# Order of a two-layer decoder's fp32r kernel on one core: formed weight blocks kept behind the sums, strict product order in the last two blocks, last key copies first, third row block's output operands earlier

## The chip, the cores and the metric

One NeuronCore of a Trainium2 chip runs the whole program. The metric is the device time of one execution in microseconds (us); the kernel before took 2277.39 us (median of 3 runs, 2275.31 to 2277.57). Less is better. A measurement of this kernel can tell about 0.2% (4.6 us) from no change.

## What is computed

Two layers over 1024 tokens of width 1024 in fp32. Layer 0 mixes by latent attention (8 heads), layer 1 by differential attention (8 heads with two softmax maps each); after each stands a gated feed-forward of inner width 5632.

```python
for i in range(DEPTH):                      # 2
    mix = _mla_mixer(h, ...) if i % 2 == 0 else _diff_mixer(h, ...)
    h = _layernorm(ALPHA * h + mix, ln_mix_g[i], ln_mix_b[i])
    h = _layernorm(ALPHA * h + _swiglu(h, ffn_w_gu[i], ffn_w_down[i]), ln_ffn_g[i], ln_ffn_b[i])

def _swiglu(x, w_gu, w_down):
    gate, up = jnp.split(x @ w_gu, 2, axis=-1)
    return (jax.nn.silu(gate) * up) @ w_down

def _diff_mixer(x, ...):                    # cut
    a = p[:, 0] - lam * p[:, 1]             # p: two softmaxes over the same mask
    o = jnp.einsum('bhqk,bkhe->bqhe', a, v)
    o = _rmsnorm(o, g_sub) * (1.0 - lambda_init)
    return o.reshape(b, s, DIFF_HEADS * DIFF_V) @ w_o
```

## The kernel before

Every fp32 product is done as three fp32r matmuls: each operand is cut into a high part (a cast, on ACT) and a low part (operand less high part, on DVE or POOL), and high by high, high by low and low by high are summed in PSUM. An `op_` tile holds both parts of one weight piece. A product of four 128-row steps is 12 matmuls of 512 columns; the text calls it a unit.

**Stages**, by time in the profile: attention of layer 0 to about 345 us; its output projection to 450; gate and up product of feed-forward 0 to 871; its down product to 1086; attention of layer 1 to 1550; the rest of its output projection to 1624; gate and up of feed-forward 1 to 2044; down to the end.

**Gate and up product** (`ffn`). The weight is cut into 22 blocks n of 4 pieces (a11, a12, a21, a22: one 1 MB load `gr`, issued on SP's queue by `load`, L563). Each block takes seven units, called 1 to 7 by the `pr` of `product`, in a scheme that trades one of eight products for sums of weight pieces and of inputs. `prepare(n, pr)` forms the weight sums in place on DVE (L585, L587, L589) and the tile `s3` (L593), then cuts the piece in two (`op_unit`, L514 and L515). `consume(n, pr)` runs the unit into a PSUM tile `ga`, `gb` or `gc` and adds the result into `tmp` or `pg` on DVE (L633 to L645). `gb` is one bank: unit 7 may not write it before DVE has added unit 6's result. The inputs of the units are `xs["t1"]`, `["t2"]`, `["t3"]`, `["t4"]`, `["b22"]` (in the trace `t3h_f` and so on). `stream` lists the units and `prepare` is called four units ahead of `consume`. The first six blocks' units 1 and 2 run early (`gates`, from loads `gp` by `load_pre`, tiles `gp`/`op_gp`/`pg`). `pending` is the transposition of the last row block of the output projection (`raw_x`, PE tiles `xTp_a`).

**The order** on each engine is set ahead of time by a scheduler that simulates the program with its own costs, priorities and tile slots; each engine then runs its list strictly in that order. SP's list is the DMA queue: a load that waits holds back those behind it. `behind(i, j)` pins instruction i after j. `big_tile` gives one of six 1 MB slots, shared by `gr`, `pg`, `hp`, `sh` and others.

**Down product.** `t2` subtracts two weight tiles in place (`tt`, DVE) and cuts the result; `from_h` cuts the activations (`op_h`).

**Attention of layer 1.** `proj_b` makes a head's queries and keys; keys are copied as high part on ACT (`bk`, L1350) and low part on DVE (L1351), in two column halves `hf` and two map halves `mp`. `score_b` (`s_b`) and the softmax (`l_b` exponentials, L227) follow; row blocks of the last head go in `LAST_ORDER` = 6, 7, 4, 5, 2, 3, 0, 1. `OutProj` begins the output projection under the last head: `of` loads six heads' outputs of a row block (`of_a`), and cuts them into `oh_a`, `ol_a` (ACT L405, DVE L406); `product` runs them against the weights `wo`, `who`, `wlo` into `zp_a`; `rest` finishes the row blocks, of the third and later ones also the cutting.

Of the kernel before, what the change touches and what calls it, by code (L numbers as in the profile page):

```python
# [12 lines left out]
ALU = mybir.AluOpType  # L13
# [3 lines left out]
P = 128  # L17
# [25 lines left out]
def trunk(  # L43
# [84 lines left out]
    def load_w(src, cols, name, hi=None, lo=None, eng=None, raw=None, ins=False):  # L128

        if raw is None:  # L130
            raw = wp.tile([P, 1024], F32, tag="wr", bufs=2, name=f"r_{name}")
        nc.sync.dma_start(raw[:, :cols], src)
        if hi is None:
            hi = wp.tile([P, 1024], F32R, tag="wh", name=f"h_{name}")
            lo = wp.tile([P, 1024], F32R, tag="wl", name=f"l_{name}")
        A.copy(hi[:, :cols], raw[:, :cols])
        j = (eng or G).tensor_tensor(lo[:, :cols], raw[:, :cols], f32(hi[:, :cols]), ALU.subtract)
        return (hi, j.ins) if ins else (hi, lo)

# [7 lines left out]
    def tr(ps_out, in_):  # L147
        T.transpose(ps_out, in_, ident)

# [135 lines left out]
    def out_proj(side, w_o, o_dram, x_src, x_dst, lng, lnb, xo):  # L285


        with tc.tile_pool(name="op0", bufs=2, side=side, reuse_waits="tile") as pool:
# [21 lines left out]
            for tb in LAST_ORDER:  # L310
# [34 lines left out]
                prev = (tb, y)  # L345
        return lambda: raw_x(prev[1], xo, prev[0], f"a0_{prev[0]}")

    class OutProj:
# [24 lines left out]

        def of(self, tb):

# [10 lines left out]
            else:  # L386
# [13 lines left out]
            self.sums[tb] = small(f"sum_{nm}", 2)  # L400
            self.split(tb, slice(0, n), of)

        def split(self, tb, hs, o):
            oh, ol = (t[:, hs] for t in self.oh[tb])
            A.activation(oh, o, AF.Copy, scale=self.scale)  # L405
            V.scalar_tensor_tensor(ol, o, self.scale, f32(oh), ALU.mult, ALU.subtract)  # L406
# [37 lines left out]
        def rest(self, lng, lnb, xo):  # L444
# [15 lines left out]
            self.st.close()  # L460
            return lambda: raw_x(self.z[prev], xo, prev, f"a1_{prev}")

    def raw_x(y, xo, tb, name):

# [4 lines left out]
        for kh in range(2):  # L469
            pt = ps_s(f"xTp_{name}_{kh}")  # L470
            for k in range(4):
                tr(pt[:, k * P:(k + 1) * P], y[:, (4 * kh + k) * P:(4 * kh + k + 1) * P])
            pv = pt.rearrange("p (k t) -> p k t", k=4)
# [6 lines left out]
        if tb < 4:  # L480
# [40 lines left out]
    def ffn(side, xo, xst, pending, layer, x_src, x_dst, lng, lnb, next_x, spare=()):  # L521
# [43 lines left out]
        def load_pre(n, eng):  # L565
# [7 lines left out]
        begun = set()  # L573

        def prepare(n, pr):


            if n not in begun:
                begun.add(n)
                load(n + 1)  # L580
                if n < npre - 1:
                    load(n + 2)
            a11, a12, a21, a22 = (r[n][:, i] for i in range(4))
            if pr == ("5" if n < 2 else "6"):
                V.tensor_tensor(a21, a21, a22, ALU.add)  # L585
            if pr == ("3" if n < 2 else "6"):
                V.tensor_tensor(a11, a21, a11, ALU.subtract)  # L587
            if pr == "3":
                V.tensor_tensor(a12, a12, a11, ALU.subtract)  # L589
# [8 lines left out]
            eng = V if n < 2 else eng  # L598
            ops[n, pr] = op_unit(src, eng, f"g{layer}_{n}_{pr}")

        def consume(n, pr):
# [3 lines left out]
            if pr in "12":  # L605
# [26 lines left out]
            if pr == "6":  # L632
                V.tensor_tensor(u2, p1, acc[n, "b"], ALU.add)  # L633
                for c in acc[n, "cs"] if n < 2 else ():
                    V.tensor_tensor(u2, u2, c, ALU.add)
            elif pr == "7":
                V.tensor_tensor(u3, p1, acc[n, "b"], ALU.add)  # L637
                if n < 2:
                    V.tensor_tensor(u3, u3, acc[n, "cs"][0], ALU.add)
            elif pr == "5":  # L640
                V.tensor_tensor(u3, u3, acc[n, "c"], ALU.add)  # L641
            elif pr == "4":
                V.tensor_tensor(p1, p1, acc[n, "b"], ALU.add)
            else:
                V.tensor_tensor(u2, u2, acc[n, "c"], ALU.add)  # L645
            if pr == ("4" if n < 2 else "3"):
# [639 lines left out]
    with ExitStack() as st:  # L1286
# [37 lines left out]
        def proj_b(h, which, hf):  # L1324
            if (which, h) not in wts:
                wts[which, h] = load_w(w_b_qk[h, which], 1024, f"wb{h}_{which}")
            wh, wl = wts[which, h]
            hs = slice(hf * 512, hf * 512 + 512)
# [16 lines left out]
            else:  # L1345
                for mp in range(2):
                    a = slice(mp * 64, mp * 64 + 64)
                    b = slice(64 - mp * 64, 128 - mp * 64)
                    k = kt[h % 2][:, mp]
                    A.copy(k[a, hs], m[a, :])  # L1350
                    V.tensor_tensor(k[b, hs], m[a, :], f32(k[a, hs]), ALU.subtract)  # L1351
# [218 lines left out]
```

## Time and profile before

| | |
|---|---|
| median of 3 runs | 2277.39 us (2275.31 to 2277.57) |
| the profiled execution | 2276.84 us |
| its span | 2275.1 us (1.7 us lie outside) |
| DVE busy | 1569.9 us (69%) |
| ACT busy | 1022.1 us (45%) |
| POOL busy | 869.2 us (38%) |

The page gives for each engine the time in which it ran an instruction; the trace's timeline gives the start of each instruction, its length and, in square brackets, the idle time of the engine ahead of it with the instruction (or transfer) that ended it. The list of waits sums those by line. A table by windows gives the busy time in each window and, as PEclk, the share of full speed that TensorE's clock was granted there.

### The profile page before, as it was taken

How to read it: one execution, taken by the hardware profiler on the slowest of the kernel's cores; microseconds unless marked ns; L12 is line 12 of the kernel's file. 1: busy time of each engine (PE TensorE's matmuls, PEld its weight loads, DVE VectorE, ACT ScalarE, POOL GpSimd, SP SyncE). 2: the span in 40 equal slices, each digit the busy share in tenths (PEclk: the TensorE clock that was granted, in tenths of full speed). 3: DMA queues.
4: the chain of work that ended last, by engine and by line, in shares of the span. 5: the costliest groups of instructions: out<-in, count | busy, mean ns of one | idle time of the engine just before them, and what ended most of it. 6: DMA issues, size and time to landing. Idle time of an engine off the chain costs nothing.

```text
span 2275.1 us, 31209 instructions
## 1 busy us (share of the span) xinstructions
PE 2238.8 (98%) x11410; PEld 1915.3 (84%) x11410; DVE 1569.9 (69%) x2848; ACT 1022.1 (45%) x2115; POOL 869.2 (38%) x693
## 2 busy tenths in 40 slices
PE   8999999999999999999999999999999999999998
PEld 8899998887888888888889898987778888888886
DVE  5676665696666667878576667677786656658878
ACT  4455664342333333445465656555432333334444
POOL 2232341113444444656333534322014444445551
PEclk9999999999999999999999999999999999999999
DMA  5010115443535338454311212054343223238453
GB/s 203 14 35 31 51 61 188 145 156 103 183 128 195 125 130 324 176 199 148 103 44 32 70 33 67 20 202 167 111 171 117 92 102 107 100 124 311 164 180 149
DMA packets 110443, 287.77 MB, mean 126 GB/s; under 512 B 8513, under 2 KB 30657, under 8 KB 99793
## 3 DMA queue, kind: packets, MB, share of 16 engines
q1 hardware_dynamic: 105872, 275.35, 34.2%
q0 software_dynamic: 4416, 10.42, 1.7%
q8 instruction: 90, 1.47, 0.3%
q14 instruction: 65, 0.52, 0.1%
HBM read 204.47 MB, written 77.07 MB: 124 GB/s over the span
## 4 chain that ended last, share of the span: by engine, by line
PE 87%; DVE 6%; DMA 3%; issue 2%; ACT 1%; POOL 1%; SPq 0%; DVEq 0%; POOLq 0%; ACTq 0%
PE gb L551 14%; PE gc L551 10%; PE ga L551 8%; PE dw L843 6%; PE zp_a L417 4%; PE s_a L219 4%; PE s_b L219 3%; PE dv L843 3%; PE bp L143 3%; PE bp L145 3%; PE dx L843 3%; PE bp L144 3%; PE dy L843 2%; PE o_a L262 2%; PE o_b L262 2%
## 5 line engine op out<-in xcount | busy, mean ns | idle before, releaser
L514 ACT CAST op_g<-gr 128x512 fp32r<-128x512 f32 x240 | 146.8, 621 | 378.6 <-PE gb L551 185.3
L515 POOL TENSOR_TENSOR op_g<-gr,op_g 128x512 fp32r<-128x512 f32 x104 | 145.7, 1406 | 248.7 <-ACT op_g L514 144.5
L515 DVE TENSOR_TENSOR op_h<-rh,op_h 128x512 fp32r<-128x512 f32 x152 | 169.5, 1144 | 48.3 <-ACT op_h L514 48.3
L551 PE MATMUL ga<-xh_m,op_g 128*128 128x512 f32 x512 | 168.3, 389 | 0.0
L514 ACT CAST op_h<-rh 128x512 fp32r<-128x512 f32 x152 | 92.6, 620 | 152.0 <-PE dx L843 50.4
L843 PE MATMUL dw<-op_w_t,op_h 128*128 128x512 f32 x660 | 151.6, 390 | 0.6 <-DVE op_h L515 0.6
L843 PEld LDWEIGHTS dw<-op_w_t,op_h 128*128 128x128 f32 x660 | 123.6, 188 | 26.8 <-DVE op_h L515 1.4
L515 POOL TENSOR_TENSOR op_w_t<-tt,op_w_t 128x512 fp32r<-128x512 f32 x66 | 101.8, 1551 | 84.5 <-ACT op_w_t L514 83.0
L227 ACT ACTIVATE l_b<-l_b,mx_b 128x256 f32<-128x256 f32 (+7 forms) x128 | 99.4, 777 | 66.8 <-DVE mx_b L222 65.3
L515 DVE TENSOR_TENSOR op_g<-gr,op_g 128x512 fp32r<-128x512 f32 x136 | 112.6, 832 | 16.9 <-ACT op_g L514 16.6
L515 POOL TENSOR_TENSOR op_g<-s,op_g 128x512 fp32r<-128x512 f32 x40 | 55.1, 1376 | 179.5 <-ACT op_g L514 171.4
L551 PE MATMUL gb<-t3h_f,op_g 128*128 128x512 f32 x352 | 117.9, 397 | 5.5 <-DVE tmp L633 5.5
L843 PE MATMUL dx<-op_w_b,op_h 128*128 128x512 f32 x528 | 121.1, 390 | 0.8 <-DVE op_w_b L515 0.8
L1367 POOL TENSOR_SCALAR l_b<-l_b,rb,cst 128x128 f32<-128x128 f32 (+3 forms) x64 | 52.6, 821 | 179.2 <-DVE rb L1366 171.8
L843 PEld LDWEIGHTS dx<-op_w_b,op_h 128*128 128x128 f32 x528 | 98.9, 188 | 22.4 <-DVE op_w_b L515 1.7
L551 PE MATMUL gb<-t4h_f,op_g 128*128 128x512 f32 x352 | 115.7, 390 | 1.3 <-DVE tmp L637 1.3
L551 PE MATMUL gc<-b22h_f,op_g 128*128 128x512 f32 x352 | 115.8, 390 | 0.8 <-DVE tmp L641 0.6
L551 PE MATMUL gb<-t2h_f,op_g 128*128 128x512 f32 x352 | 115.7, 390 | 0.4 <-DVE op_g L515 0.4
L551 PE MATMUL gc<-t1h_f,op_g 128*128 128x512 f32 x352 | 115.9, 390 | 0.0
L551 PEld LDWEIGHTS ga<-xh_m,op_g 128*128 128x128 f32 x512 | 96.2, 188 | 19.9
L143 PE MATMUL bp<-xT_f,h_wb 128*128 128x512 f32 x256 | 100.8, 394 | 0.1
L145 PE MATMUL bp<-xT_f,l_wb 128*128 128x512 f32 x256 | 100.7, 393 | 0.0
(391 smaller groups left out, 6753.5 us busy)
## 6 DMA issues: line engine op xcount, KB each, us to landing
gr<-in_w_gu SPq DMA_DIRECT2D x44, 1024.0 KB, 6.8
rh<-h_dr SPq DMA_DIRECT2D x28, 1024.0 KB, 4.9
h_dr<-sh SPq DMA_DIRECT2D x22, 1024.0 KB, 4.9
h_dr<-hp SPq DMA_DIRECT2D x22, 768.0 KB, 4.1
tt<-in_w_dn SPq DMA_DIRECT2D x44, 256.0 KB, 6.3
wo_dr<-op_pwo SPq DMA_DIRECT2D x16, 512.0 KB, 3.4
z<-xs_dr SPq DMA_DIRECT2D x16, 512.0 KB, 8.2
rw_b<-in_w_dn SPq DMA_DIRECT2D x8, 1024.0 KB, 7.7
```

Source lines behind the costliest of these rows:

```text
L143: T.matmul(ps_out, lh, rh, start=(i == 0), stop=False)
L144: T.matmul(ps_out, lh, rl, start=False, stop=False)
L145: T.matmul(ps_out, ll, rh, start=False, stop=(i == n - 1))
L219: T.matmul(s[:, :w], lh, rh[:, ks], start=(j == 0), stop=(j == len(q_pass) - 1))
L227: ends["exp"] = A.activation(l[:, :n], l[:, :n], AF.Exp, bias=mx, scale=-1.0, accum_out=sm).ins
L262: T.matmul(po[:, c], a, b[:, j % 2, c], start=st, stop=sp_, skip_group_check=True)
L417: T.matmul(m, a[:, h, :], self.wo[h][w][:, c], start=(start and h == heads[0] and a is oh and w == 0), stop=(stop and h == heads[-1] and a ...
L514: turns["hi"] = A.copy(t[:, 0], src).ins
L515: turns["last"] = eng.tensor_tensor(t[:, 1], src, f32(t[:, 0]), ALU.subtract).ins
L551: i = T.matmul(o, w[:, a, kc], x[b][:, k, :], start=(first and k == 0 and (a, b) == (0, 0)), stop=(k == 3 and a == 1), skip_group_check=Tr ...
L843: T.matmul(o, h[:, a, c], w[:, b_], start=(first and (a, b_) == (0, 0)), stop=(last and a == 1), skip_group_check=True,).ins for a, b_ in ...
L1367: G.tensor_scalar(l1[:, :n], l1[:, :n], r[:, 1:2], nlam, ALU.mult, ALU.mult)
```

## The change

It alters order alone, in seven places; the counts of matmuls, adds, casts and transfers stay as they are.

1. `product`: blocks 20 and 21 run their units strictly in the order of the program; before, block 21 alone.
2. `prepare`: the DVE adds that form weight sums go through `formed`, which pins each behind `allowed[-1]`: at first the last add of the pending row block's transposition, later the sum of the unit six back (`added_up`, `marks`).
3. `prepare`: the 1 MB load of block n+2 is issued for every n (before, for n below 5), that of n+3 for n below 4.
4. Layer 1: only blocks 0 and 1 are loaded and cut by `load_pre` before `gates(0)`, blocks 2 and 3 after it; the cast of block 3 stands behind the copy of `p1`; the last row block's first transposes stand behind the last unit of `gates(0)`.
5. `t2`: its subtractions stand behind the low part of the activation unit (`turns["h"]`).
6. `proj_b`: the first head's query weight has its low part (POOL) behind the second row block's normalization; in the last head the second half's key copy of columns 0 to 511 on ACT stands ahead of the exponentials.
7. `OutProj`: the cutting is a function of its own, `turned`, called for the third row block (row block 4) under the last head.

```diff
-                    if n == NFF - 1 and k == 0 and (a, b) == (0, 0) and "product" in ends:
+                    if n >= 20 and k == 0 and (a, b) == (0, 0) and "product" in ends:
                         behind(i, ends["product"])
...
+                if layer and n == 3:
+                    behind(turns["hi"], ends["p1"])
...
+        def formed(*args):
+            i = V.tensor_tensor(*args).ins
+            if allowed:
+                behind(i, allowed[-1])
...
                 load(n + 1)
-                if n < npre - 1:
-                    load(n + 2)
+                load(n + 2)
+                if n < npre - 2:
+                    load(n + 3)
...
-                V.tensor_tensor(a21, a21, a22, ALU.add)
+                formed(a21, a21, a22, ALU.add)
...
-        for n in range(4):
+        for n in range(4 - 2 * layer):
             load_pre(n, G if n < 2 else V)
         gates(0)
+        for n in range(4 - 2 * layer, 4):
+            load_pre(n, V)
         load(0)
         load(1)
         with tc.high_priority(40):
-            pending()
+            turned = pending(ends["product"])
...
+        allowed.append(turned)
         for u in stream[:2]:
             prepare(*u)
...
         for i, u in enumerate(stream):
+            if i >= 6 and marks[i - 6]:
+                allowed.append(marks[i - 6])
             if i + ahead < len(stream):
                 prepare(*stream[i + ahead])
             consume(*u)
+            marks.append(summed[-1] if summed else None)
...
-                    V.tensor_tensor(tt[j][:, i], r, tt[j][:, i], ALU.subtract)
+                    behind(V.tensor_tensor(tt[j][:, i], r, tt[j][:, i], ALU.subtract).ins, turns["h"])
...
+                if (h, which) == (0, 0):
+                    behind(ends["low"], normed[1][2])
...
-                    A.copy(k[a, hs], m[a, :])
+                    i = A.copy(k[a, hs], m[a, :]).ins
+                    if (h, hf, mp) == (H - 1, 0, 1):
+                        behind(ends["exp"], i)
...
         at(b, begin_out)
+        at(b + 7, lambda: proj[0].turned(LAST_ORDER[2], ends["exp"]))
```

**Place one: feed-forward 0, blocks 2 to 5, about 504 to 516 us before.** DVE's list before (`gr0_5` is the block's raw pieces, `tmp0_2` the sums of block 2):

```order
L515 TENSOR_TENSOR op_g0_3_6_5849<-gr0_3_5604,op_g0_3_6_5849 128x512
L663 TENSOR_TENSOR hp0_0_5757<-pg0_0_5321 128x512
L585 TENSOR_TENSOR gr0_5_5845<-gr0_5_5845 128x512
L587 TENSOR_TENSOR gr0_5_5845<-gr0_5_5845 128x512
L589 TENSOR_TENSOR gr0_5_5845<-gr0_5_5845 128x512
L633 TENSOR_TENSOR tmp0_2_5830<-tmp0_2_5830,gb0_2_5829 128x512
L593 TENSOR_TENSOR s3_0_5_6059<-gr0_5_5845 128x512
```

The same place of DVE's list now (L592 is the add in `formed`, L624 that in `added_up`, L528 and L688 what L515 and L663 were):

```order
L528 TENSOR_TENSOR op_g0_3_6_5851<-gr0_3_5583,op_g0_3_6_5851 128x512
L688 TENSOR_TENSOR hp0_0_5759<-pg0_0_5321 128x512
L624 TENSOR_TENSOR tmp0_2_5832<-tmp0_2_5832,gb0_2_5831 128x512
L592 TENSOR_TENSOR gr0_4_5606<-gr0_4_5606 128x512 x2
L624 TENSOR_TENSOR tmp0_3_5927<-tmp0_3_5927,gb0_3_5926 128x512
L592 TENSOR_TENSOR gr0_5_5738<-gr0_5_5738 128x512
```

SP's queue there before:

```order
L682 DMA pg_dr0_5320<-pg0_4_5501 128x2048
L655 DMA tmp0_2_5830<-pg_dr0_5320 128x1024
L655 DMA tmp0_3_5925<-pg_dr0_5320 128x1024
L563 DMA gr0_5_5845<-in_w_gu 128x2048
L674 DMA h_dr0_0_5309<-hp0_0_5757 128x3x512
```

and now:

```order
L707 DMA pg_dr0_5320<-pg0_4_5501 128x2048
L576 DMA gr0_4_5606<-in_w_gu 128x2048
L576 DMA gr0_5_5738<-in_w_gu 128x2048
L680 DMA tmp0_2_5832<-pg_dr0_5320 128x1024
L680 DMA tmp0_3_5927<-pg_dr0_5320 128x1024
L699 DMA h_dr0_0_5309<-hp0_0_5759 128x3x512
```

The sum of block 2's unit 6 went ahead of block 5's three adds, and block 5's load ahead of the two loads of `tmp`.

**Place two: start of feed-forward 1, about 1627 to 1635 us before.** PE's list before, from the last matmuls of `gates(0)`'s unit 1 of block 1 (`ga1_1`) on; `xTp_a1_1` are the transposes of the last row block:

```order
L551 MATMUL ga1_1_16268<-xl0_m1_15593,op_gp1_1_1_16231 128x512
L551 MATMUL ga1_1_16268<-xh0_m1_15592,op_gp1_1_1_16231 128x512
L148 MATMUL xTp_a1_1_0_16312<-ident_60,z_a1_0_16027 128x128 x4
L148 MATMUL xTp_a1_1_1_16317<-ident_60,z_a1_0_16027 128x128 x4
L551 MATMUL ga1_0_16254<-xh1_m1_15594,op_gp1_0_2_16226 128x512
L551 MATMUL ga1_0_16254<-xl1_m1_15595,op_gp1_0_2_16226 128x512
```

and now (between the second and the third row the 24 matmuls of unit 2 of blocks 0 and 1):

```order
L564 MATMUL ga1_1_16251<-xl0_m1_15598,op_gp1_1_1_16231 128x512
L564 MATMUL ga1_1_16251<-xh0_m1_15597,op_gp1_1_1_16231 128x512
...
L564 MATMUL ga1_1_16251<-xl1_m1_15600,op_gp1_1_2_16234 128x512
L564 MATMUL ga1_1_16251<-xh1_m1_15599,op_gp1_1_2_16234 128x512
L149 MATMUL xTp_a1_1_0_16312<-ident_60,z_a1_0_16029 128x128 x4
L149 MATMUL xTp_a1_1_1_16317<-ident_60,z_a1_0_16029 128x128 x4
```

The transposes moved behind two units, which are 24 matmuls.

**Place three: end of the last head, about 1545 to 1553 us before.** ACT's list before (`zp_a1_6` are squares of row block 6 for its layer norm, `sq7_0` and `sqr7_0` belong to the last head's normalization):

```order
L250 CAST pth_b7_0_0_15494<-pt_b7_1_0_15538 128x2x128
L170 ACTIVATE zp_a1_6_0_6_15545,ssq_a1_6_15606<-z_a1_6_15013,nmu_a1_6_15603 128x512
L170 ACTIVATE zp_a1_6_1_6_15553,ssq_a1_6_15606<-z_a1_6_15013,nmu_a1_6_15603 128x512
L1394 ACTIVATE sq7_0_15569<-bo_10214 128x512
L1396 CAST sqr7_0_15570<-sq7_0_15569 128x512
L405 ACTIVATE oh_a1_4_15665<-of_a1_4_15663,cst_58 128x768
L405 ACTIVATE oh_a1_4_15665<-bo_10214,cst_58 128x256
```

and now:

```order
L228 ACTIVATE l_b7_1_1_15453,smb7_1_15444<-l_b7_1_1_15453,mx_b7_1_1_0_15457 128x256
L414 ACTIVATE oh_a1_4_15480<-of_a1_4_15478,cst_58 128x768
L1446 ACTIVATE sq7_2_15439<-ms7_2_0_15472,cst_58 128x256
L251 CAST pth_b7_0_0_15499<-pt_b7_0_0_15497 128x128
L1448 ACTIVATE sq7_2_15439<-sq7_2_15439 128x256
L251 CAST pth_b7_0_0_15499<-pt_b7_1_0_15543 128x2x128
L414 ACTIVATE oh_a1_4_15480<-bo_10214,cst_58 128x256
L171 ACTIVATE zp_a1_6_0_6_15550,ssq_a1_6_15611<-z_a1_6_15015,nmu_a1_6_15608 128x512
L171 ACTIVATE zp_a1_6_1_6_15558,ssq_a1_6_15611<-z_a1_6_15015,nmu_a1_6_15608 128x512
```

The cutting of row block 4 (`oh_a1_4`) stands ahead of the last casts of the softmax (`pth_b7_0_0`) and of row block 6's squares, and no longer behind `sqr7_0`. On PE the 24 matmuls of `zp_a1_4_0_0` follow directly on `zp_a1_7_1_6`, and `ms7_0_0` comes after them.

More of the change, by code (lines that the diff above doesn't have):

```diff
@@ L137, in load_w @@
         j = (eng or G).tensor_tensor(lo[:, :cols], raw[:, :cols], f32(hi[:, :cols]), ALU.subtract)
+        ends["low"] = j.ins
         return (hi, j.ins) if ins else (hi, lo)
@@ L345, in out_proj @@
                 prev = (tb, y)
-        return lambda: raw_x(prev[1], xo, prev[0], f"a0_{prev[0]}")
+        return lambda after: raw_x(prev[1], xo, prev[0], f"a0_{prev[0]}")
     class OutProj:
@@ L372, in __init__, with turned @@
                     self.wo.append([x.bitcast(F32R) for x in t])
-        def of(self, tb):
+        def turned(self, tb, after=None):
             nm, n = f"a1_{tb}", self.HEADS
@@ L392, in of @@
             self.oh[tb] = [t.rearrange("p (h q) -> p h q", h=H) for t in hl]
+            self.split(tb, slice(0, n), of, after)
+        def of(self, tb):
+            nm = f"a1_{tb}"
+            k = LAST_ORDER.index(tb)
+            first = k < 2
+            if tb not in self.oh:
+                self.turned(tb)
             if first:
@@ L400, in of, with split @@
             self.sums[tb] = small(f"sum_{nm}", 2)
-            self.split(tb, slice(0, n), of)
-        def split(self, tb, hs, o):
+        def split(self, tb, hs, o, after=None):
             oh, ol = (t[:, hs] for t in self.oh[tb])
-            A.activation(oh, o, AF.Copy, scale=self.scale)
+            i = A.activation(oh, o, AF.Copy, scale=self.scale).ins
+            if after is not None:
+                behind(i, after)
             V.scalar_tensor_tensor(ol, o, self.scale, f32(oh), ALU.mult, ALU.subtract)
@@ L460, in rest, with raw_x @@
             self.st.close()
-            return lambda: raw_x(self.z[prev], xo, prev, f"a1_{prev}")
-    def raw_x(y, xo, tb, name):
+            return lambda after: raw_x(self.z[prev], xo, prev, f"a1_{prev}", after)
+    def raw_x(y, xo, tb, name, after=None):
         c = slice((tb % 4) * P, (tb % 4) * P + P)
@@ L471, in raw_x @@
             for k in range(4):
-                tr(pt[:, k * P:(k + 1) * P], y[:, (4 * kh + k) * P:(4 * kh + k + 1) * P])
+                i = tr(pt[:, k * P:(k + 1) * P], y[:, (4 * kh + k) * P:(4 * kh + k + 1) * P])
+                if k == 0 and after is not None:
+                    behind(i, after)
             pv = pt.rearrange("p (k t) -> p k t", k=4)
@@ L485, in raw_x @@
             V.tensor_tensor(b21, b21, pvs[1], ALU.subtract)
-            V.tensor_tensor(b21, b21, b12, ALU.add)
+            return V.tensor_tensor(b21, b21, b12, ALU.add).ins
     def new_x(pools, name):
@@ L571, in load_pre @@
                 ops[n, pr] = op_unit(t[:, i], eng, f"gp{layer}_{n}_{pr}")
-        begun = set()
+                if layer and n == 3:
+                    behind(turns["hi"], ends["p1"])
+        begun, summed, allowed = set(), [], []
+        def formed(*args):
+            i = V.tensor_tensor(*args).ins
+            if allowed:
+                behind(i, allowed[-1])
         def prepare(n, pr):
@@ L580, in prepare @@
                 load(n + 1)
-                if n < npre - 1:
-                    load(n + 2)
+                load(n + 2)
+                if n < npre - 2:
+                    load(n + 3)
             a11, a12, a21, a22 = (r[n][:, i] for i in range(4))
             if pr == ("5" if n < 2 else "6"):
-                V.tensor_tensor(a21, a21, a22, ALU.add)
+                formed(a21, a21, a22, ALU.add)
             if pr == ("3" if n < 2 else "6"):
-                V.tensor_tensor(a11, a21, a11, ALU.subtract)
+                formed(a11, a21, a11, ALU.subtract)
             if pr == "3":
-                V.tensor_tensor(a12, a12, a11, ALU.subtract)
+                formed(a12, a12, a11, ALU.subtract)
             s3 = None
@@ L592, in prepare @@
                 s3 = wp.tile([P, 2, 512], F32, tag="wr", name=f"s3_{layer}_{n}", bufs=2)[:, 0]
-                V.tensor_tensor(s3, a22, a11, ALU.subtract)
+                formed(s3, a22, a11, ALU.subtract)
             src, eng = {
@@ L599, in prepare, with added_up @@
             ops[n, pr] = op_unit(src, eng, f"g{layer}_{n}_{pr}")
+        def added_up(*args):
+            summed.append(V.tensor_tensor(*args).ins)
         def consume(n, pr):
@@ L612, in consume @@
                 if pr == "1":
-                    A.copy(p1, acc[n, "a"])
+                    ends["p1"] = A.copy(p1, acc[n, "a"]).ins
                 else:
@@ L632, in consume @@
             if pr == "6":
-                V.tensor_tensor(u2, p1, acc[n, "b"], ALU.add)
+                added_up(u2, p1, acc[n, "b"], ALU.add)
                 for c in acc[n, "cs"] if n < 2 else ():
-                    V.tensor_tensor(u2, u2, c, ALU.add)
+                    added_up(u2, u2, c, ALU.add)
             elif pr == "7":
-                V.tensor_tensor(u3, p1, acc[n, "b"], ALU.add)
+                added_up(u3, p1, acc[n, "b"], ALU.add)
                 if n < 2:
-                    V.tensor_tensor(u3, u3, acc[n, "cs"][0], ALU.add)
+                    added_up(u3, u3, acc[n, "cs"][0], ALU.add)
             elif pr == "5":
-                V.tensor_tensor(u3, u3, acc[n, "c"], ALU.add)
+                added_up(u3, u3, acc[n, "c"], ALU.add)
             elif pr == "4":
-                V.tensor_tensor(p1, p1, acc[n, "b"], ALU.add)
+                added_up(p1, p1, acc[n, "b"], ALU.add)
             else:
-                V.tensor_tensor(u2, u2, acc[n, "c"], ALU.add)
+                added_up(u2, u2, acc[n, "c"], ALU.add)
             if pr == ("4" if n < 2 else "3"):
@@ L773, in from_h @@
                     t = op_unit(src, V, f"h{layer}_{name}_{j}", tags, pool)
+                    turns["h"] = turns["last"]
                     if late and j > 1:
@@ L1349, in proj_b @@
                     k = kt[h % 2][:, mp]
-                    A.copy(k[a, hs], m[a, :])
+                    i = A.copy(k[a, hs], m[a, :]).ins
+                    if (h, hf, mp) == (H - 1, 0, 1):
+                        behind(ends["exp"], i)
+                        ends["key"] = i
                     V.tensor_tensor(k[b, hs], m[a, :], f32(k[a, hs]), ALU.subtract)
```

3 lines of the change are left out of this document (2 added, 1 removed).

## The prediction

> **What bounds the kernel now.** I read the head of the profile first, then the list of TensorE's waits, then the timeline at each wait that is long, then the clock in narrow windows.
>
> ```profile
> span 2275.1 us, 31209 instructions
> PE 2238.8 (98%) x11410; PEld 1915.3 (84%) x11410; DVE 1569.9 (69%) x2848; ACT 1022.1 (45%) x2115; POOL 869.2 (38%) x693
> ```
>
> PE has work in 2238.8 of 2275.1 us. An edit of order that leaves all 11410 matmuls can win at most the 36.3 us in which PE stands, and what PE loses at a low clock. The list of waits says where it stands (engine, line, what it waited for, total, times, longest):
>
> ```profile
> PE gb L551 <- DVE tmp L633: 5.5, 2, 2.7
> PE xTp_a L148 <- DVE z_a L183: 2.0, 1, 2.0
> PE gb L551 <- DVE tmp L637: 1.3, 1, 1.3
> PE s_b L219 <- DVE bk L1351: 1.3, 1, 1.3
> PE xTp_f L148 <- DVE y_f L183: 0.8, 1, 0.8
> PE zp_a L417 <- DVE oh_a L406: 0.7, 1, 0.7
> PE gc L551 <- DVE tmp L641: 0.6, 1, 0.6
> PE ms L1404 <- ACT sqr L1396: 0.4, 1, 0.4
> PE zp_a L417 <- ACT oh_a L405: 0.3, 1, 0.3
> ```
>
> The largest is one pattern that comes twice, once in each feed-forward. Its first place, on DVE, SP and PE:
>
> ```profile
> 484.00 0.33 SPq L682 DMA_DIRECT2D pg_dr<-pg  x1
> 499.09 3.27 SPq L655 DMA_DIRECT2D tmp<-pg_dr  x2
> 503.96 0.33 SPq L563 DMA_DIRECT2D gr<-in_w_gu  x1
> 509.47 0.39 PE L551 MATMUL gb<-t2h_f,op_g 128*128 128x512 f32 x1
> 509.92 0.39 PE L551 MATMUL gb<-t2h_f,op_g 128*128 128x512 f32 x1
> 512.19 0.39 PE L551 MATMUL gb<-t2l_f,op_g 128*128 128x512 f32 x1
> 510.67 1.81 DVE L585 TENSOR_TENSOR gr<-gr 128x512 f32<-128x512 f32 x1 [2.41 <-DMA gr<-in_w_gu]
> 512.52 1.65 DVE L587 TENSOR_TENSOR gr<-gr 128x512 f32<-128x512 f32 x1
> 514.20 0.69 DVE L589 TENSOR_TENSOR gr<-gr 128x512 f32<-128x512 f32 x1
> 514.81 0.68 DVE L633 TENSOR_TENSOR tmp<-tmp,gb 128x512 f32<-128x512 f32 x1
> ```
>
> Block 2's unit 6 ended at 509.47 + 0.39 = 509.86, but its sum (L633) began only at 514.81. DVE had been idle for 2.41 us, waiting for block 5's load, issued at 503.96; then it did three adds for block 5, 4.1 us, which stand ahead of the sum in its list. Unit 7 cannot write its bank until the sum is done, and PE stood. From 509.92 to 512.19 there are ten matmul starts: 0.227 us each, so a unit of 12 takes 2.72 us. In feed-forward 1 it is the same:
>
> ```profile
> 1695.64 1.72 DVE L585 TENSOR_TENSOR gr<-gr 128x512 f32<-128x512 f32 x1 [2.51 <-DMA gr<-in_w_gu]
> ```
>
> After the long stalls the clock falls. In the rows of windows the granted clock is the last column but two (1.00 is full speed):
>
> ```profile
> 516.00:518.00 2.00, 2.00 (x8) 1.55 (x7) 1.29 (x3) 0.00 (x0) 0.00 (x0) 0.63 0.47 197
> 518.00:520.00 2.00, 2.00 (x7) 1.55 (x6) 0.00 (x0) 0.00 (x0) 0.00 (x0) 0.52 0.00 0
> 1632.00:1634.00 2.00, 2.00 (x10) 1.66 (x9) 0.78 (x2) 0.52 (x1) 0.00 (x0) 0.67 0.98 397
> 1634.00:1636.00 2.00, 2.00 (x6) 1.61 (x5) 0.85 (x2) 2.00 (x5) 0.00 (x0) 0.50 0.94 328
> 1700.00:1702.00 2.00, 1.58 (x5) 1.27 (x6) 2.00 (x4) 0.00 (x0) 0.00 (x0) 0.74 0.89 282
> 1702.00:1704.00 2.00, 2.00 (x6) 1.52 (x5) 0.16 (x1) 0.00 (x0) 0.00 (x0) 0.50 0.57 238
> 844.00:848.00 4.00, 2.70 (x12) 1.97 (x11) 2.89 (x3) 1.24 (x2) 3.98 (x3) 1.00 0.54 211
> ```
>
> At half speed 0.63 means 1.48 us of the 2, and 0.52 means 1.92: together 3.4 us, in which half the work is lost, 1.7 us. So a stall of 2.7 us costs 4.4. The stall of 2.0 us at 1630 is followed by the same; the one of 1.3 us at 845 isn't (1.00).
>
> **The change part by part.** Sums are made against the profiled execution, 2276.84 us (span 2275.1, 1.7 outside), which lies 0.55 below the median of 2277.39.
>
> *Formed adds and earlier loads (parts 2 and 3).* By the new DVE list the sum of block 2's unit 6 comes right behind `hp`, ahead of all of block 5's adds; it can start when PE is done, about 509.9, and end at 510.6, long before PE wants the bank at 512.6. Apart from that, block 5's load now follows the `pg_dr` store of 484.00 on SP's queue: 20 us earlier than 503.96. Either alone takes away the stall. Gain: 5.5 in both layers plus 2 x 1.7 of clock, **8.9**. What covers the moved adds is the distance: a block's adds may stand up to ten units (27 us) before use. If that cover is gone, the stall is that of the next sum (first rival).
>
> *Last row block in layer 1 (part 4).* PE now has two more units, 5.4 us, ahead of the transposes it waited 2.0 us for.
>
> ```profile
> 1630.20 1.28 DVE L183 SCALAR_TENSOR_TENSOR z_a<-z_a,rs_a,gb 128x1024 f32<-128x1024 f32 x1 [0.44 <-POOL rs_a L180]
> ```
>
> Their input is ready at 1630.20 + 1.28 = 1631.48; PE had come 2.0 us before that, and now comes at 1629.5 + 5.4 = 1634.9. Gain 2.0 + 1.7 of clock, **3.7**. Late next is the DVE chain behind the transposes, begun some 3 us later. By the list its users stand some 20 us behind, after the other gate units, so I cost it at nothing; at worst it returns the whole 3.
>
> *Strict order in block 20 (part 1).* The stall of 1.3 us in feed-forward 0:
>
> ```profile
> 837.41 3.00 POOL L515 TENSOR_TENSOR op_g<-gr,op_g 128x512 fp32r<-128x512 f32 x2 [9.31 <-DVE tmp L645]
> 840.44 1.76 DVE L587 TENSOR_TENSOR gr<-gr 128x512 f32<-128x512 f32 x1 [1.19 <-POOL op_g L515]
> 845.53 0.68 DVE L637 TENSOR_TENSOR tmp<-tmp,gb 128x512 f32<-128x512 f32 x1
> ```
>
> DVE waited for POOL, then formed block 21, and the sum came late. In the new order another unit, 2.7 us, stands between unit 7 and unit 4. Gain between 0 and 1.3; I take **1.0**. Feed-forward 1 has the like at `gc`, 0.6, of which I take **0.4**.
>
> *First head's query weight (part 6).*
>
> ```profile
> 1087.75 2.41 POOL L137 TENSOR_TENSOR l_wb<-r_wb,h_wb 128x1024 fp32r<-128x1024 f32 x1 [9.65 <-ACT h_wb L136]
> 1090.70 1.29 DVE L183 SCALAR_TENSOR_TENSOR y_f<-y_f,rs_f,gb_f 128x1024 f32<-128x1024 f32 x1 [1.55 <-POOL rs_f L180]
> ```
>
> The 2.41 us on POOL go behind the little root that DVE waited 1.55 us for; PE's 0.8 us go with it: **0.8**. The low part is then wanted later than it is made, hidden by the value products on PE; without them it would cost up to 2.4.
>
> *Second key copy (part 6).*
>
> ```profile
> 1496.35 1.14 ACT L227 ACTIVATE l_b<-l_b,mx_b 128x1024 f32<-128x1024 f32 x1
> 1497.86 0.58 ACT L1350 CAST bk<-bp 64x512 fp32r<-64x512 f32 x1
> 1504.48 0.73 PE L417 MATMUL zp_a<-wo,oh_a 128*128 128x512 f32 x2 [0.68 <-DMA wo<-wo_dr]
> ```
>
> The copy comes 1.1 us sooner, and PE's wait of 1.3 shrinks. But six microseconds on, PE waits for the weights `wo`, and their load isn't moved: PE arrives there sooner and stands longer. Between 0 and 1.3 I take **0.3**.
>
> *Third row block (part 7).*
>
> ```profile
> 1549.87 0.93 ACT L405 ACTIVATE oh_a<-of_a,cst 128x768 fp32r<-128x768 f32 x1
> 1550.84 1.37 DVE L406 SCALAR_TENSOR_TENSOR oh_a<-of_a,cst,oh_a 128x768 fp32r<-128x768 f32 x1
> ```
>
> PE's waits for `oh_a` on DVE and ACT and for `sqr`, 0.7 + 0.3 + 0.4 = 1.4, have their operands made some 5 us before. The same 0.93 us on ACT now stands ahead of the softmax's last casts, and can delay them by as much. Between -0.9 and 1.4 I take **1.2**.
>
> *The down product's order (part 5)* names no wait of the list; I cost it at nothing, with 0.5 us either way.
>
> The sum is 8.9 + 3.7 + 1.0 + 0.4 + 0.8 + 0.3 + 1.2 = 16.3. Against it: units and adds change places in the whole of both gate and up stages, and each move can meet a wait of the small kind (0.3 to 0.7 in the list). Not seen in the trace; bounded by nothing and by a dozen such, 8 us, I take **3.0**, near the lower end since the moved work has many microseconds of lead. Net 13.3: the profiled execution would take 2263.5, the median **2264.1 us**.
>
> **The rivals.**
>
> *Slower: adds run at their slow length ahead of sums.* The same add of 128x512 takes 0.69 and 1.81 us in the rows above. If the adds now pinned behind one sum run slow and stand ahead of the next, 1.8 + 1.7 + 0.7 = 4.2 us, a sum is late wherever that exceeds the 2.7 us of the unit between plus what DVE has spare. It decides from about 3.4 us of adds in one row. At 0.5 to 0.6 us in each of 44 blocks it would cost 24, less the 16.3: **2285 us**. Against it: by the new list two adds at most stand between two sums at place one, and DVE is idle 31% of the time.
>
> *The stalls of block 5 stay.* If the load's transfer, put earlier into the crowded queue, delays `tmp` instead, the 8.9 remain: gain 13.3 - 8.9 = 4.4, **2273 us**. Against: block 5's load would be issued near 484, 15 us ahead of the `tmp` loads (499.09).
>
> *The clock does not follow the stalls.* Then 5.1 of the sum are missing and the gain is 8.2: **2269 us**. For it: only three cases. The three low spells begin at 516.5, 1632.7 and 1701.0, that is 1116.2 and 68.3 us apart. [...]
>
> *The change doesn't do what it says.* Out by the lists of order: sum, load and transposes did move.
>
> **How the numbers follow.** Forecast as above, 2258 to 2269: 0.68. More than that: 0.04. Clock apart, 2269: 0.10. Block 5 stays, 2273: 0.12. Slower, 2285: 0.06. Leaving out the slower case and some of the worst ends, the range is 2257 to 2274; the bounds of the terms give 2259 without new waits (18.5 us won), and with 8 us of them and each term at its low end 2274 (11.2 - 8 = 3.2 us won); two us below the first are left for small waits that may go as well. Faster by over 0.2% (4.6 us, about what a measurement of this kernel can tell; below 2272.8): 0.68 + 0.04 + 0.10 and a quarter of the block 5 case, 0.85. The rest of that case, 0.09, is within 0.2%. Slower: 0.06.
>
> **What would show it.** In the profile after: no `gb` wait of 2.7 for `tmp`, DVE's add for block 5 without the wait for the load, no clock below 1.00 near 517, 1633 and 1701, `xTp_a` without wait, `y_f` within 0.2, longer waits at `wo`. It would be wrong if PE's idle time outside these places grew by over 5 us, or if the sums began to come late in each block.

## The result, and the profile after

The changed kernel took 2256.72 us (median of 4 runs, 2256.08 to 2257.14) against 2277.06 us before (median of 4, 2275.31 to 2277.57). The ratio is 0.9915, with a 95% interval of 0.9901 to 0.993: faster by 20.3 us. The prediction had said 2264.1, with a range of 2257 to 2274; the direction was right, the gain half as large again as forecast, and the median lies 0.3 us under the range.

The head of the page of the kernel after; the profiled execution took 2256.08 us, 20.8 less than the one before:

```profile
span 2254.3 us, 31238 instructions
PE 2230.0 (99%) x11410; PEld 1912.1 (85%) x11410; DVE 1535.4 (68%) x2848; ACT 1024.1 (45%) x2115; POOL 860.4 (38%) x693
PE 96%; DVE 2%; issue 1%; ACT 1%; DMA 0%; POOL 0%; SPq 0%; DVEq 0%; POOLq 0%; ACTq 0%
```

The same 11410 matmuls now keep PE busy in 99% of the span, and the chain that ended last runs through PE for 96% of it (87% before). The list of PE's waits of the kernel after, in the rows that answer to those of before:

```profile
PE gb L564 <- DVE tmp L624: 1.5, 2, 0.9
PE s_b L220 <- DVE mx_b L223: 1.1, 2, 0.6
PE zp_a L428 <- DVE ptl_b L252: 0.9, 1, 0.9
PE dx L876 <- DVE op_w_b L528: 0.8, 2, 0.5
PE bp L144 <- DVE bvl L1353: 0.4, 1, 0.4
```

Gone are the two waits of 2.7 us, the 2.0 us for `z_a`, those for `bk`, `y_f`, `oh_a` and `sqr`. Two of 0.9 and 0.7 us for a sum in `tmp` have come, one of 0.4 for `bvl`, and those for `mx_b` (0.2 before) and `ptl_b` (0.3 before) have grown. The place of the first long stall, in the timeline of SP and DVE of the kernel after:

```profile
484.40 4.85 SPq L576 DMA_DIRECT2D gr<-in_w_gu  x2
507.91 1.78 DVE L688 TENSOR_TENSOR hp<-pg 128x512 f32<-128x512 f32 x1
509.61 0.68 DVE L624 TENSOR_TENSOR tmp<-tmp,gb 128x512 f32<-128x512 f32 x1
510.21 3.17 DVE L592 TENSOR_TENSOR gr<-gr 128x512 f32<-128x512 f32 x2
513.30 0.68 DVE L624 TENSOR_TENSOR tmp<-tmp,gb 128x512 f32<-128x512 f32 x1
```

The loads of blocks 4 and 5 are issued from 484.40 on, and DVE does the sum at 509.61, right behind `hp` and 0.2 us after PE ended the unit (509.39); it was at 514.81 before. The windows of the kernel after around the old spells of half clock (granted clock in the last column but two):

```profile
516.00:520.00 4.00, 4.00 (x19) 3.31 (x18) 4.00 (x8) 0.62 (x1) 0.00 (x0) 1.00 0.86 330
1620.00:1628.00 8.00, 8.00 (x41) 6.69 (x40) 6.00 (x10) 6.87 (x12) 0.00 (x0) 1.00 0.81 299
```

Full clock in both, and the trace has no spell of half clock at all between its first 12 and its last 8 us. From the starts of the matmuls one can take, for each kernel, the time by which a start comes later than its usual distance from the one ahead (the median for that pair of matmul shapes in the profile). Over the whole program that sum is 64.5 us before and 43.7 after; the difference, 20.8, is the whole gain of the two profiled executions. The rest of the working uses this sum by place ("by the starts"); it is a little more than the list of waits gives for the same stall.

### The profile page after: what moved, and what is told of

The parts are those of the page before. It is cut to its first block, busy times and chain, and to the rows that moved or that the text cites. A ratio compares the mean times of both kernels' runs of the same rounds, so it can differ in the third digit from the quotient of the medians.

```text
span 2254.3 us, 31238 instructions
## 1 busy us (share of the span) xinstructions
PE 2230.0 (99%) x11410; PEld 1912.1 (85%) x11410; DVE 1535.4 (68%) x2848; ACT 1024.1 (45%) x2115; POOL 860.4 (38%) x693
## 4 chain that ended last, share of the span: by engine, by line
PE 96%; DVE 2%; issue 1%; ACT 1%; DMA 0%; POOL 0%; SPq 0%; DVEq 0%; POOLq 0%; ACTq 0%
PE gb L564 16%; PE ga L564 11%; PE gc L564 11%; PE dw L876 7%; PE dx L876 5%; PE zp_a L428 4%; PE s_a L220 4%; PE s_b L220 3%; PE dv L876 3%; PE dy L876 3%; PE bp L144 3%; PE bp L146 3%; PE bp L145 3%; PE o_a L263 2%; PE o_b L263 2%; PE hq L1093 1%
## 5 line engine op out<-in xcount | busy, mean ns | idle before, releaser
L528 POOL TENSOR_TENSOR op_g<-gr,op_g 128x512 fp32r<-128x512 f32 x104 | 142.0, 1369 | 250.3 <-ACT op_g L527 189.9
L528 DVE TENSOR_TENSOR op_h<-rh,op_h 128x512 fp32r<-128x512 f32 x152 | 160.3, 1072 | 77.1 <-ACT op_h L527 77.0
L592 DVE TENSOR_TENSOR gr<-gr 128x512 f32<-128x512 f32 x132 | 121.7, 922 | 85.1 <-POOL op_g L528 85.0
L624 DVE TENSOR_TENSOR tmp<-tmp,gb 128x512 f32<-128x512 f32 x120 | 81.8, 683 | 132.8 <-PE gb L564 128.5
L528 POOL TENSOR_TENSOR op_w_t<-tt,op_w_t 128x512 fp32r<-128x512 f32 x66 | 96.0, 1460 | 97.6 <-ACT op_w_t L527 89.7
L528 DVE TENSOR_TENSOR op_g<-gr,op_g 128x512 fp32r<-128x512 f32 x136 | 116.1, 857 | 17.5 <-ACT op_g L527 17.2
L528 POOL TENSOR_TENSOR op_g<-s,op_g 128x512 fp32r<-128x512 f32 x40 | 55.8, 1395 | 158.4 <-ACT op_g L527 150.9
```

The lines of the kernel that those rows point to most:

```text
L528: turns["last"] = eng.tensor_tensor(t[:, 1], src, f32(t[:, 0]), ALU.subtract).ins
L592: i = V.tensor_tensor(*args).ins
L624: summed.append(V.tensor_tensor(*args).ins)
```

## The experiments

The theory after the result: PE stood where a sum on DVE was late, either because adds for a later block stood ahead of it behind a late load, or because units 7 and 4 of one block were neighbours on PE; a long stall then also halved the clock (0.50 granted in the kernel before, for 3.4 us behind each of three stalls). Rivals: the earlier loads and not the pin did it; the clock does not follow the stalls; the strict order removed a wait by itself. Nine kernels are the changed one with something undone; one has part 2 alone; two go on from it. The kernel before, run beside them on the same chip, took 2276.9, 2276.5 and 2276.1 us in the three sets; the changed kernel was not run again in them. A difference of about 1 us in time is therefore not told from one between the sets, and such cases rest on the waits in the profiles.

**u_both: parts 2 and 3 undone.**

```diff
-            if allowed:
-                behind(i, allowed[-1])
...
-                load(n + 2)
-                if n < npre - 2:
-                    load(n + 3)
+                if n < npre - 1:
+                    load(n + 2)
```

> The kernel after with the pin of the formed adds taken out and the loads as before. Theory (three adds of block 5 stand behind a late load and ahead of a sum; each such stall of 2.9 us draws 3.4 us at half clock): both gb waits of 2.7 come back, 5.8 us, with two spells of half clock, 3.1 us: about 2265.6 us. Rival (the clock does not follow the stalls): the waits come back without the spells, about 2262.5. Rival (other parts took the stalls away): 2257 and no gb wait of 2.7.

It took 2270.83 us (2269.10 to 2273.61, 9 runs), 14.1 more than the changed kernel and 5.2 more than expected. Two waits of its list:

```profile
PE gb L564 <- DVE tmp L621: 6.6, 4, 2.7
PE ga L564 <- DVE xr_m L497: 2.9, 1, 2.9
```

The two long `gb` waits are back (with the two short ones 6.6 us), and one of 2.9 us is new, at the start of feed-forward 1: without the pin, block adds stand there ahead of the last row block's transposition, which part 4 moved later. Its windows, at the first stall and at the new one:

```profile
512.00:516.00 4.00, 1.26 (x6) 0.76 (x5) 3.93 (x5) 0.62 (x1) 1.83 (x2) 1.00 1.08 348
516.00:520.00 4.00, 4.00 (x19) 3.27 (x19) 2.67 (x5) 0.62 (x1) 0.00 (x0) 1.00 0.31 131
1638.00:1640.00 2.00, 0.52 (x2) 0.48 (x3) 2.00 (x5) 2.00 (x5) 0.00 (x0) 1.00 1.03 406
1640.00:1642.00 2.00, 2.00 (x7) 1.55 (x6) 2.00 (x4) 2.00 (x5) 0.00 (x0) 0.66 0.53 221
```

The stall of 2.7 us at 513, alike to the hundredth to that of the kernel before, was this time followed by full clock (1.00), while the new one drew a spell (0.66). So neither theory on the clock held as it was put: a stall of that length may draw a spell, and need not.

**u_formed: part 2 undone, the earlier loads kept.** Only the first two removed lines of the diff above.

> The kernel after with the pin of the formed adds alone taken out; the loads stay one block earlier. Theory (either alone takes the stall away): no gb wait of 2.7, 2256.7 to 2258. Rival (the pin does the work, the loads nothing): 4.4 to 8.9 us more, 2261 to 2266. A third outcome: adds now stand in other places ahead of sums and a few waits of 0.5 to 1 come, 2258 to 2260.

2263.16 us (2262.10 to 2264.56), 6.4 more. There is no `gb` wait of 2.7, so at that place the loads alone suffice, as predicted. But at the start of feed-forward 1 stands this, in its timeline of SP, DVE and PE:

```profile
1623.39 1.31 SPq L576 DMA_DIRECT2D gr<-in_w_gu  x2
1629.95 1.42 DVE L592 TENSOR_TENSOR gr<-gr 128x512 f32<-128x512 f32 x2 [5.55 <-DMA gr<-in_w_gu]
1633.10 0.68 DVE L495 TENSOR_TENSOR xr_m<-xTp_a,xr_m 128x512 f32<-128x512 f32 x1
1634.90 0.68 DVE L497 TENSOR_TENSOR xr_m<-xr_m,xTp_a 128x512 f32<-128x512 f32 x1
1635.72 0.77 PE L564 MATMUL ga<-xh_m,op_gp 128*128 128x512 f32 x1 [3.20 <-DVE xr_m L497]
```

It is the same picture as the first stall before: DVE idle for 5.55 us at a load, with the adds that need the load ahead of work that PE wants; PE stood for 3.2 us, and its clock was halved for 6.8 us after: the next matmuls, at 1636.29 and 1636.71, took 0.63 us each, those ahead of the stall 0.39, and the granted clock of the run was 0.997 (0.998 in the changed kernel's profile). The time lies in the rival's range, but not by its mechanism, and none of the three outcomes named this place; the pin is needed there.

**u_loads: part 3 undone, the pin kept.** The last lines of the first diff alone.

> The kernel after with the loads as before; the pin of the formed adds stays. Theory (either alone takes the stall away): no gb wait of 2.7 on tmp, 2256.7 to 2258; DVE still waits some 2 us for block 5's load, behind the sums. Rival (the loads do the work, the pin nothing): 4.4 to 8.9 us more, 2261 to 2266.

2256.86 us (2256.07 to 2257.29): 0.1 from the changed kernel. The earlier loads win nothing beside the pin. The expected wait of DVE for block 5's load did not come either. How the pin works is seen in DVE's list of instructions, first before, then in the changed kernel (count | busy us, mean ns | idle us ahead of them and what ended it):

```profile
L585 DVE TENSOR_TENSOR gr<-gr 128x512 f32<-128x512 f32 x44 | 41.6, 946 | 17.5 <-DMA gr<-in_w_gu 17.5
L592 DVE TENSOR_TENSOR gr<-gr 128x512 f32<-128x512 f32 x132 | 121.7, 922 | 85.1 <-POOL op_g L528 85.0
```

Before, DVE stood 17.5 us for loads of blocks, in 14 waits; with the pin no such wait is left, in the changed kernel as in u_loads and p_pin. Without it the waits are back whether the loads are early (u_formed, 14.3 us) or not (u_both, 17.0 us).

**p_pin: the kernel before with part 2 alone.** The diff of `formed`, `allowed`, `marks` and `added_up` in the section on the change, and no other part.

> The kernel before with part 2 alone (the pin of the formed adds). Theory: both gb waits of 2.7 on tmp go and with them the spells of half clock that they drew; the wait for z_a (2.2) and the others stay. 5.8 us plus 0 to 3.1 of clock, plus 0.7 where block 20's units 7 and 4 no longer stand together in feed-forward 0: 2267 to 2270.5. Rival (the pin needs the earlier loads or the later transposes): 2273 or more.

2264.63 us (2261.56 to 2265.99, ratio 0.9946, interval 0.9929 to 0.9962): 12.4 of the 20.3 us by the medians (11.4 against the kernel before in its own set), more than expected. Rows of its list of waits:

```profile
PE xTp_a L149 <- DVE z_a L184: 2.0, 1, 2.0
PE dw L871 <- DVE op_h L528: 1.4, 2, 0.8
PE gc L564 <- DVE tmp L621: 1.3, 2, 0.6
PE s_b L220 <- DVE bk L1381: 1.3, 1, 1.3
```

No `gb` wait for `tmp` is left at all; what parts 4 to 6 touch still waits (`z_a`, `bk`, and `dw`, which has grown from 0.6 to 1.4). Four small stalls of before, of 0.4, 0.2, 0.5 and 0.6 us by the matmul starts (463, 599, 657 and 1657 us), went as well (of the last 0.1 is left), which the prediction had not put down to any part. Two spells of half clock are left in its profile (granted clock of the run 0.997), one behind the wait for `z_a` and one at 1545 us, behind the waits that part 7 touches.

**u_last: part 4 undone.**

```diff
-        for n in range(4 - 2 * layer):
+        for n in range(4):
...
-            turned = pending(ends["product"])
+            turned = pending(None)
```

> The kernel after with part 4 undone (all four early blocks cut ahead, the last row block's transposes where the scheduler puts them). Theory: PE's wait for z_a of 2.2 us and its spell of half clock, 1.6 us, come back, and the two small waits near 1657 of the kernel before, 0.6: 2256.7 + 3.8 to 4.4 = 2260.5 to 2261.1. Rival (the wait comes back without a spell of half clock): 2259. Rival (other parts shifted it away): 2257.

2261.0 us (2260.53 to 2261.13), 4.3 more, as the theory had it in size; but not in kind. In its list of waits:

```profile
PE xTp_a L149 <- DVE z_a L184: 2.0, 1, 2.0
PE gc L564 <- ACT op_g L527: 0.8, 3, 0.3
```

and its window behind the first of them:

```profile
1622.00:1626.00 4.00, 4.00 (x19) 3.33 (x18) 3.54 (x6) 4.00 (x9) 0.00 (x0) 1.00 1.01 357
```

The wait of 2.0 us is back without a spell; four small waits of 0.3 to 0.5 us behind it (1.6 by the starts) make it 3.8. The agreement in time is luck.

**u_strict: part 1 undone**, **v_6: strict order from block 6 on**, **v_57: block 19's unit 5 pinned as well.** The condition in `product` of u_strict, v_6 and v_57, in this order, beside that of the changed kernel:

```diff
-                    if n >= 20 and k == 0 and (a, b) == (0, 0) and "product" in ends:
+                    if n == NFF - 1 and k == 0 and (a, b) == (0, 0) and "product" in ends:
```

```diff
-                    if n >= 20 and k == 0 and (a, b) == (0, 0) and "product" in ends:
+                    if n >= 6 and k == 0 and (a, b) == (0, 0) and "product" in ends:
```

```diff
-                    if n >= 20 and k == 0 and (a, b) == (0, 0) and "product" in ends:
+                    if (n >= 20 or n == 19 and x is xs["t1"]) and k == 0 and (a, b) == (0, 0) and "product" in ends:
```

The two waits left in the changed kernel belong to block 19. In its timeline of PE and DVE, feed-forward 0:

```profile
819.30 0.39 PE L564 MATMUL gb<-t3h_f,op_g 128*128 128x512 f32 x1
819.73 0.69 DVE L624 TENSOR_TENSOR tmp<-tmp,gb 128x512 f32<-128x512 f32 x1 [1.07 <-PE gb L564]
820.56 0.47 PE L564 MATMUL gb<-t4h_f,op_g 128*128 128x512 f32 x1 [0.87 <-DVE tmp L624]
```

DVE is idle and begins as soon as unit 7 (`t3h`) ends; unit 4 (`t4h`) is simply next in PE's list and must wait for the sum. The strict order of block 20 pushed the units that had stood between them behind.

> The kernel after with strict order in block 21 alone, as before. By its list unit 4 no longer stands next to unit 7 in block 19, but in feed-forward 1 it does in block 20. Theory (a unit 4 directly behind unit 7 of its block waits 0.8 to 1.0 us for the sum, wherever that pair stands): the waits of 1.0 and 0.8 in block 19 go, one of 1.0 comes in block 20 of feed-forward 1, none in block 20 of feed-forward 0: 0.8 us less than the kernel after, 2255.9. Rival (the strict order did remove the wait of 1.5 in block 20): that one comes back, 2257.3 or more.

2257.0 us (2256.44 to 2257.72), 0.3 more. Block 19's two waits went and one came in feed-forward 1 as expected:

```profile
PE gb L564 <- DVE tmp L624: 1.1, 1, 1.1
```

but another of 0.8 us (`gc` at unit 3 of block 20 in feed-forward 0), which the list does not foretell, gave back the gain (by the starts 1.8 us went and 2.0 came). Part 1 by itself is worth nothing that these runs can tell.

> The kernel after with strict order from block 6 on. By its list a whole unit 5 stands between units 7 and 4 in every one of these blocks. Theory (the pair 7, 4 is what waits): no wait of gb for tmp, both waits of block 19 go: 1.8 us less than the kernel after, 2254.9. Rival (the free order of the middle blocks hid other waits): small waits in many of 16 x 2 blocks, 0.3 each, 2260 or more.

2260.84 us (2259.75 to 2262.99), 4.1 more: the forecast fell. PE and DVE in feed-forward 0, at block 5:

```profile
552.33 1.66 DVE L592 TENSOR_TENSOR s<-gr 128x512 f32<-128x512 f32 x1
554.51 0.67 DVE L624 TENSOR_TENSOR tmp<-tmp,gb 128x512 f32<-128x512 f32 x1
555.24 0.50 PE L564 MATMUL gb<-t4h_f,op_g 128*128 128x512 f32 x1 [2.27 <-DVE tmp L624]
```

The pair 7, 4 now stands at the seam, in block 5, and DVE was also in the middle of adds: 2.3 us in each feed-forward, each with a spell of half clock in the profiled execution, the slowest of the four (granted clock of that run 0.997; at 555.81 a matmul took 0.49 us, ahead of the wait 0.39). In the blocks behind there is no wait of 0.2 us or more, so the rival (free order hides many waits) fell as well.

> The kernel after with block 19's unit 5 also pinned behind its unit 7, so that a whole unit stands between 7 and 4 in blocks 19 to 21 and, by the list, in no later block are the two neighbours. Theory: both remaining gb waits, 1.0 and 0.8 us, go and none comes: 2254.9. Rival (a wait comes at the next seam, block 18): 2256 to 2257.

2255.09 us (2253.91 to 2256.02, ratio 0.9907, interval 0.9893 to 0.9922). In its list of waits no `gb` wait for `tmp` is left, and behind the start the largest rows, beside two of 0.5 us each for `op_w_b`, are these:

```profile
PE s_b L220 <- DVE mx_b L223: 1.1, 2, 0.6
PE zp_a L144 <- ACT ob L1255: 1.0, 1, 1.0
```

The median is 1.6 us under the changed kernel's, about the 1.8 expected; the intervals of the two ratios overlap, so the waits' going is shown, and the time only likely. By its median it is the fastest kernel of the study.

**u_t2: part 5 undone.**

```diff
-                    behind(V.tensor_tensor(tt[j][:, i], r, tt[j][:, i], ALU.subtract).ins, turns["h"])
+                    V.tensor_tensor(tt[j][:, i], r, tt[j][:, i], ALU.subtract)
```

> The kernel after with part 5 undone (the subtractions of the down stage's t2 where the scheduler puts them; PE's list is unchanged). Theory: two small waits of PE in the down stages, 0.4 and 0.5 us, come back: 2257.6. Rival (they went with the shift of everything else): 2256.7.

2257.88 us (2257.32 to 2258.57), 1.2 more. One `dw` wait is back, 0.7 us by the starts, with PE's own list unchanged; the other, and the rest of the 1.2, are not shown.

**u_turned: part 7 undone.**

```diff
-        at(b + 7, lambda: proj[0].turned(LAST_ORDER[2], ends["exp"]))
```

> The kernel after with part 7 undone (third row block's operands made in the rest of the output projection). Theory: PE's waits there grow from 1.5 to 3.1 us as before: 2258.2. Rival (the copies under the last head cost what they win): 2256.7.

2259.19 us (2257.44 to 2261.48), 2.5 more, where 1.5 was expected. Its waits, and a window behind them:

```profile
PE zp_a L428 <- DVE oh_a L417: 0.7, 1, 0.7
PE ms L1442 <- ACT sqr L1434: 0.4, 1, 0.4
PE zp_a L428 <- ACT oh_a L414: 0.3, 1, 0.3
1546.00:1548.00 2.00, 2.00 (x7) 1.52 (x6) 2.00 (x4) 0.81 (x3) 0.86 (x1) 0.50 0.81 217
```

The three waits are those of before, to the tenth. Here, in the slowest of the four runs, they drew a spell of half clock, which they did not in the profile of the kernel before.

**u_key and u_qw: the two halves of part 6 undone**, the first two removed lines in u_qw, the third in u_key.

```diff
-                if (h, which) == (0, 0):
-                    behind(ends["low"], normed[1][2])
...
-                        behind(ends["exp"], i)
```

> The kernel after with the second key copy of the last head again where the scheduler puts it. Theory: PE's waits from the first scores of the last head to the first output product add up to 3.3 us as before, against 2.1: 2257.9. Rival (the transfer of wo ends at the same time either way, so what is won ahead of it is lost at it): 2256.7.

2257.64 us (2256.52 to 2258.93), 0.9 more. The late starts there add up to 3.1 us against 2.1, of them 0.6 at `wo`, as the theory has it. But the rival is not out. In the traces of all eleven kernels that have the copy in its new place, the first piece of `wo` lands 7.8 to 9.0 us after its issue. In five, the changed kernel among them, it lands by 7.9 us, before PE arrives or just as it does, and the sum is 2.1; in the other six it takes 8.4 us or more, PE waits 0.6 to 1.2 us for it, and the sum is 2.7 to 3.3. With the copy in its old place (the kernel before, p_pin, u_key) it is 3.1 to 3.4. So in six of eleven executions the transfer takes back half or more of what is won ahead of it.

> The kernel after with the low part of the first query weight again ahead of the normalization's root on POOL. Theory: PE's wait at the first transposes of attention B is 1.0 us again against 0.6: 2257.1. Rival: no change in that wait, 2256.7.

2257.02 us in its one run. The wait for `y_f` is back (1.0 us by the starts), against 0.6 after it in the changed kernel; a single time cannot tell 0.4 us.

## Why the prediction was right, and where not

- **The two stalls of 2.7 us, 8.9.** Right in mechanism: late adds behind a late load, ahead of a sum. They went with 5.8 us by the starts and 3.1 of clock, where 5.5 and 3.4 were forecast: a spell costs 1.6 us, not 1.7, and the two errors cancel. "Either alone takes away the stall" holds at that place (u_formed, u_loads), but the pin also guards another, which u_formed shows, and the earlier loads are not needed at all.
- **Last row block, 3.7.** Right: the wait for `z_a` went, 2.2 us by the starts, and the spell behind it, 1.6. Luck has a part in both terms: they count a spell behind each stall as certain, and u_both had the stall of 2.7 us, u_last that of 2.0, without one. That the DVE chain behind it would have room holds only with the pin (u_both, u_formed).
- **Strict order, 1.0 and 0.4.** Wrong in part. The waits in block 20 went, 1.5 and 0.8 us by the starts; 1.0 and 0.8 came at block 19, where the pin leaves 7 and 4 side by side. Net 0.4, and even that is not of part 1: in p_pin, which lacks it, the 1.5 had already shrunk to 0.8. I had looked only at the block that was pinned, not at its neighbour.
- **Query weight, 0.8.** It won 0.4: `y_f` no longer waits, the next product waits 0.4 us for `bvl`.
- **Key copy, 0.3.** It won 1.2 in the profile after (3.3 us of late starts to 2.1), since the wait at `wo` that was to take it back did not occur in that execution. It did in six others, between 0.6 and 1.2 us (u_key): the end of that transfer varies. Over the eleven profiles the gain averages some 0.6, nearer to the forecast than the 1.2 of this one.
- **Third row block, 1.2.** 1.5 by the starts; u_turned adds the clock.

These terms measure 16.2 us by the starts and were forecast at 16.3. The step that failed is the next: "Against it: units and adds change places ... I take 3.0". In both gate and up stages only the two waits at block 19 came, 1.8 us, which are already taken off above; beyond them nothing stood against it. Instead some 4.6 us more went: the four small waits that p_pin removed, 1.7; two in the down stages, 0.9 (u_t2 brings one back); about 1.3 in the start right behind each stall, which is late by another 0.1 us (35 such starts before, 22 after); and the rest, some 0.7, in starts late by less than 0.3 us each. I had bounded the new waits "by nothing and by a dozen such" and never from the side on which a better order of DVE removes small waits too, though the text left two microseconds for it at the low end of the range. The high end, 2274, was not each term at its low end either: its 11.2 us leave out the 3 us that the last row block could return and the 2.4 us of the query weight.

The rival "adds run at their slow length" fell: the 176 adds that form weight sums took 182.7 us before and 164.3 after, and the list of PE's waits has none for a sum in `tmp` outside block 19. "The clock does not follow the stalls" was half right, as the last section shows.

## What to carry to other kernels

When an engine that runs its list in order waits for a load (DVE here, 17.5 us in 14 waits), ask what stands behind the waiting instruction; keeping such work behind the result that the bottleneck wants cost nothing and won some 12 us, while issuing the load sooner won nothing on top. A strict order imposed on some blocks moves the unfavourable pair to the seam: read the order at the neighbour of the pinned range, too. And bound the sum of small waits on both sides, since an edit that steadies one engine's order can remove more of them than its list of targets names.

## What was not expected of the hardware

**A stall of one length drew a spell of half clock in one profile and none in another.** A spell of the kernel before lasts 3.4 us by the windows (0.50 throughout from 516.52 to 519.94, from 1632.68 to 1636.10 and from 1700.95 to 1704.37 us). PE's wait as its list gives it, and the granted clock of the windows at its end and behind it, in four profiles:

| profile, PE waits for | wait | windows, us | granted clock |
|---|---|---|---|
| before, `tmp` | 2.7 us | 516 to 518, 518 to 520 | 0.63, 0.52 |
| u_both, `tmp` | 2.7 us | 512 to 516, 516 to 520 | 1.00, 1.00 |
| before, `tmp` | 2.7 us | 1700 to 1702, 1702 to 1704 | 0.74, 0.50 |
| u_both, `xr_m` | 2.9 us | 1638 to 1640, 1640 to 1642 | 1.00, 0.66 |
| before, `z_a` | 2.0 us | 1632 to 1634, 1634 to 1636 | 0.67, 0.50 |
| u_last, `z_a` | 2.0 us | 1618 to 1622, 1622 to 1626 | 1.00, 1.00 |
| before, `sqr`, `oh_a` twice | 0.4 + 0.3 + 0.7 us | 1548 to 1552, 1552 to 1556 | 1.00, 1.00 |
| u_turned, `sqr`, `oh_a` twice | 0.4 + 0.3 + 0.7 us | 1544 to 1546, 1546 to 1548, 1548 to 1550 | 0.94, 0.50, 0.70 |
| before, `tmp` | 1.3 us | 844 to 848, 848 to 852 | 1.00, 1.00 |

The stall of 2.7 us, that of 2.0 and the row of three short ones each stand once with a spell and once without, and the three short ones, 1.4 us in all, drew one where a single wait of 2.0 did not. So the length of the wait alone does not tell whether a spell follows; what else it depends on, these profiles do not show.

The spells go with part of the scatter as well. The mean granted clock of every run is known, and one spell more lowers it, as an estimate from the 3.4 us at half clock, by some 0.00075 (1.7 of 2275 us). Of the 26 runs of the kernel before beside the experiments, the seven at 0.995 have a median of 2278.5 us, the nine at 0.996 2277.0, and the ten at 0.997 or 0.998 2275.6: runs with more time at half clock are the longer ones. The 26 ranged over 2272.4 to 2279.3 us, the changed kernel, with no spell in its profile between its first 12 and its last 8 us, over 2256.1 to 2257.1. Three spells of 1.6 us would make 4.8 of those 6.9 us; where the spells lay in each run was not seen, as only one execution of each kernel was profiled.
